# Hybrid encoder layer on one core: two units between the seven-product pairs, and four pieces of VectorE and ScalarE work that move to later steps

## The chip, the cores and the metric

The kernel runs on one core of one Trainium2 chip. The metric is the device time of one execution, in microseconds (us), as the median of several runs. The engines have short names in the profile: PE is TensorE (the matmuls), PEld its weight loads, DVE is VectorE, ACT is ScalarE, POOL is GpSimd and SP is the sync engine, which here issues nearly all loads.

## The reference

One layer of a streaming encoder on a sequence of 256 tokens, in float32. A token-mixing sub-layer (a gated recurrence, chunked attention and a state-space branch) comes first and is not touched by the change. After it comes the part that matters here:

```python
x = x + merged @ w_out[l]                       # 2048 x 2048
h = rmsnorm(x, norm_ffn_g[l])                   # the second norm
x = x + (jax.nn.silu(h @ w_ffn_gate[l]) * (h @ w_ffn_up[l])) @ w_ffn_down[l]
return rmsnorm(x, norm_final_g)                 # the last norm
# rmsnorm(x, g): x * rsqrt(mean(x*x) + 1e-6) * g
```

x has 256 rows (two halves of 128) and 2048 columns, w_ffn_gate and w_ffn_up have 2048 x 5632 elements, and w_ffn_down 5632 x 2048.

## The kernel before

**Units and steps.** Every large matmul is cut into units. A unit is two chunks of 128 rows of a weight matrix by 512 columns (512 KB). The main loop at the end of `trunk` takes one unit per step. Because float32 accuracy is wanted from a faster matmul type, each weight w is split into `hi` (a rounded copy, made by ACT) and `lo = w - hi` (made by DVE), and each product is three matmuls: x_hi by hi, x_lo by hi, x_hi by lo. A plain ("classic") unit is four products (two chunks, two halves of tokens), so 12 matmuls of 512 columns.

**The order inside a step.** At step d the loop issues the load of unit d+5, the `hi` part of unit d+2 on ACT, then the functions put off to this step with `later(n, fn)`, then the body of unit d (the matmuls on PE), then the functions of `later_pe(n, fn)`, and last the `lo` part of unit d+2 on DVE. This program order is the order of every engine's queue: nothing is rescheduled. So an ACT or DVE instruction that has to wait holds up all that was issued behind it. `hi` and `lo` have three buffers each (`PARTB`), raw weights four (`RAWB`).

**Seven-product pairs.** In the feed-forward part (`seven_block`) some units come in pairs p0, p1, p2 that use a seven-product scheme (as Strassen's) in place of eight products: the first unit of a pair has 9 matmuls and the second 12. A pair needs more DVE work than two classic units: `Pair.mix` and `Pair.low` form differences of raw weights (tiles `praw` to `mix`), and their hi and lo (`pmix`, one buffer) as well as those of the weights used as they are. `Pair.mix` of a pair is issued three steps ahead, `Pair.high` and `Pair.low` two steps ahead. In the listings below, one pair on DVE reads: `mix<-praw`, `mix<-praw,mix` x2, `pmix<-mix,pmix`, `lo<-praw,hi` (128x512), `pmix<-mix,pmix`, `lo<-praw,hi` (128x1024).

**A feed-forward block** computes 512 hidden columns for all tokens in 16 steps. The string `FFN_ORDER` (or `FIRST_ORDER` for block 0) gives the order of its units: p for a pair's two units, g for a gate unit, u for an up unit. There are 11 blocks: 0 to 5 form part 0 and 6 to 10 part 1; after each part `down_block` multiplies the part's hidden values by w_ffn_down, with its own orders. Around the units, a block has this work, by the step in which it is issued:

- `sum1`, `sum2`, `sum3`, in the three steps after the last pair: they combine the pairs' products (tile `sg` from PSUM on ACT, adds on DVE). `after` in the code is the step after the last pair.
- `silu` at step 13: two DVE adds (`sg<-sg,mm`), each with a Silu on ACT.
- `product` at step 16, which is step 0 of the next block: two DVE adds (`acc<-acc,mm`) and then two multiplications by the norm's root and the Silu (`sg<-acc,rstd,sg`), the gating.
- `turn`: the gated values are transposed on PE (`at_ps`, four transposes of 128 x 128 at a time), in the next block at steps `after`+2 and `after`+3, and one step after each the split into `at` follows: a copy on ACT (`at<-at_ps`), and then the difference on DVE (`at<-at_ps,at`).

For the last block of a part, the transposes come at once in the `down_block`, since that uses them.

**Norms.** `square` takes the sums of squares for the second norm during the w_out product; `norm` and `rstd_of` form the root: a sum and a scale on DVE, a Sqrt on ACT, and five small DVE instructions that refine it (tiles `ss`, `scr`, `rstd`). `silu` and `product` need the result. For the last norm, `square_down` squares x by columns of 512 on ACT and then multiplies x by the gain on DVE (`x<-x,gf`). The last 10 units (`last_body`) run the first token half alone, 6 matmuls a step, and then the whole second half at once.

Of the kernel before, what the change touches and what calls it, by code (L numbers as in the profile page):

```python
# [33 lines left out]
NORM_STEP = 14  # L34
LOAD_XA = 7
NQ = 3
FFN_ORDER = 'p0 p0 g p1 p1 u p2 p2 u g g g g u u u'
FIRST_ORDER = 'g g g u u u p0 p0 g p1 p1 g g u u u'
DOWN_ORDER = ('g g g g u u u u p0 p0 g p1 p1 u p2 p2 g g g g u u u u',
              'g g g g u u u p0 p0 g p1 p1 u g g g u u u u')  # L40
# [85 lines left out]
def trunk(  # L126
# [57 lines left out]
            act.activation(dst_hi, src, AF.Identity, scale=scale)  # L184
            vec.scalar_tensor_tensor(dst_lo, src, scale, dst_hi.bitcast(F32), ALU.mult, ALU.subtract)

    def rstd_of(dst, ss, scr):

        v, t = scr[:, 0:2], scr[:, 2:4]
        vec.tensor_scalar(v, ss, 1.0 / D, EPS, ALU.mult, ALU.add)  # L190
        act.activation(t, v, AF.Sqrt)
        vec.reciprocal(dst, t)
        vec.tensor_mul(t, dst, dst)
        vec.tensor_mul(t, t, v)
        vec.tensor_scalar(t, t, -0.5, 1.5, ALU.mult, ALU.add)
        vec.tensor_mul(dst, dst, t)

    def expacc(dst, src, tmp):

# [757 lines left out]
    fx = {}  # L957
# [41 lines left out]
    for n in range(4):  # L999
        cs = slice(n * 512, (n + 1) * 512)  # L1000

        def evac_out(acc, n=n, cs=cs):
            def add():
                x2 = fx["x2"]
                for h in range(2):
                    vec.scalar_tensor_tensor(x2[:, h, cs], acc[h], 0.5, x2[:, h, cs], ALU.mult, ALU.add)
                later(1, square)
                later_pe(1, turn)

            def square():  # L1010
                sq = tp.tile([P, 2, 512], F32, tag="t", name="sq")
                for h in range(2):
                    act.activation(sq[:, h, :], fx["x2"][:, h, cs], AF.Square, accum_out=ss4[:, h, n:n + 1])
                if n == 3:
                    def norm():
                        vec.tensor_reduce(ss, ss4, AX.X, ALU.add)
                        rstd_of(rstd2, ss, scr)
                    later(1, norm)

            def turn():  # L1020
                for k0 in (4 * n, 4 * n + 2):
                    t = transpose_tokens(lambda h, k: fx["x2"][:, h, k * P:(k + 1) * P], k0, "h2_ps")

                    def parts(k0=k0, t=t):
                        h2h, h2l = fx["h2"]
                        if k0 < 2 * NQ:
                            left_sums(k0, t)
                            return
                        for i in range(2):
                            split(h2h[:, k0 + i, :], h2l[:, k0 + i, :], t[:, i * S:(i + 1) * S],  # L1030
                                  prm[:, R_G2 + k0 + i:R_G2 + k0 + i + 1])
                    later(1, parts)
            later(1, add)
        add_job(w_out, KT, n * 512, as_body(lambda: mt[0], evac_out), after_mix if n == 0 else None)
# [166 lines left out]
    def ffn_block(part, n, n0, n1):  # L1201
        def silu(b):
            t = b["sg"]
            for h in range(2):
                vec.tensor_add(t[:, h, :], t[:, h, :], b["d"][2 * h])
                act.activation(t[:, h, :], t[:, h, :], AF.Silu, scale=rstd2[:, h:h + 1])

        def product(b):
            t, u = b["sg"], fx["acc"]
            for h in range(2):  # L1210
                vec.tensor_add(u[:, h, :], u[:, h, :], b["d"][2 * h + 1])
            for h in range(2):
                vec.scalar_tensor_tensor(t[:, h, :], u[:, h, :], rstd2[:, h:h + 1], t[:, h, :], ALU.mult, ALU.mult)
            fx["turn"] = lambda k0s=(0, 2): turn(b, k0s)
            if n == n1 - 1:
                later_pe(1, fx.pop("turn"))

        def turn(b, k0s):
            kb = 4 * (n - n0)
            if part not in at:  # L1220
                at[part] = tuple(fx["fp"].tile([P, 24, S], F32R, tag=f"at{i}", name=f"at{i}") for i in range(2))
            for k0 in k0s:
                tt = transpose_tokens(lambda h, k: b["sg"][:, h, k * P:(k + 1) * P], k0, "at_ps")
                v = tt.rearrange("p (k s) -> p k s", k=2)
                ks = slice(kb + k0, kb + k0 + 2)
                later(1, lambda ks=ks, v=v: split(at[part][0][:, ks, :], at[part][1][:, ks, :], v))

        def pre(b):
            def turns():
                t = fx.pop("turn", None)  # L1230
                if t is not None:
                    t((0,))
                    later_pe(1, lambda: t((2,)))
            later_pe(b["after"] + 2, turns)

        seven_block(FIRST_ORDER if n == 0 else FFN_ORDER, KT, [(w_gate, n * 512), (w_up, n * 512)],
                    lambda: fx["h2"], lambda p: fx["sum"][:, p], (sum1, sum2, sum3), (silu, product), pre)

    def down_block(part, c, n0, n1):

        src = w_down[n0 * 512:n1 * 512]
        order = DOWN_ORDER[part]
        n_pairs = len({o for o in order.split() if o[0] == "p"})
        cg, cu = (slice((c + i) * 512, (c + i + 1) * 512) for i in range(2))

        def sum_a(b):
            x2, u = fx["x2"], fx["acc"]
            act.copy(u[:, 0], b["p1"])
            vec.tensor_add(x2[:, 0, cg], x2[:, 0, cg], u[:, 0])
            vec.tensor_add(u[:, 0], u[:, 0], b["p67"][:, 0])  # L1250

        def sum_b(b):
            x2, u = fx["x2"], fx["acc"]
            vec.tensor_add(u[:, 1], u[:, 0], b["p67"][:, 1])
            vec.tensor_add(x2[:, 1, cg], x2[:, 1, cg], u[:, 1])

        def sum_c(b):
            u = fx["acc"]
            for h in range(2):
                vec.tensor_add(u[:, h], u[:, h], b["p5"])  # L1260

        def sum_d(b):
            vec.tensor_add(fx["x2"][:, :, cu], fx["x2"][:, :, cu], fx["acc"])

        def done(col):
            def fn(b):
                x2 = fx["x2"]
                cs = (cg, cu)[col]
                for h in range(2):
                    vec.tensor_add(x2[:, h, cs], x2[:, h, cs], b["d"][2 * h + col])  # L1270
                if part == 1:
                    later(1, lambda: square_down(c + col))
            return fn

        def left(p):

            ah, al = at[part]
            w = tp.tile([P, 2, 512], F32, tag="t", name="lw")
            a = w[:, 0, :].rearrange("p (k s) -> p k s", k=2)
            sf = w[:, 1, :].rearrange("p (i s) -> p i s", i=4)  # L1280
            ks = slice(2 * p, 2 * p + 2)
            vec.tensor_add(a, ah[:, ks, :].bitcast(F32), al[:, ks, :].bitcast(F32))
            a11, a21, a12, a22 = a[:, 0, :P], a[:, 0, P:], a[:, 1, :P], a[:, 1, P:]
            vec.tensor_add(sf[:, 0], a21, a22)
            vec.tensor_sub(sf[:, 1], sf[:, 0], a11)
            vec.tensor_sub(sf[:, 2], a11, a21)
            vec.tensor_sub(sf[:, 3], a12, sf[:, 1])

            def low():
                if p < 2:  # L1290
                    t = fx["fp"].tile([P, 2, 4, P], F32R, tag="sg", name="dsum", bufs=2)
                else:
                    t = fx["sum"][:, NQ]
                dsum[part, p] = t
                act.copy(t[:, 0], sf)
                vec.tensor_sub(t[:, 1], sf, t[:, 0].bitcast(F32))
            later(1, low)

        def pre(b):
            if c == 0:  # L1300
                for p in range(n_pairs):
                    later(1 + p, lambda p=p: left(p))
                if part == 1:
                    later_pe(2, load_gain)

        seven_block(order, 4 * (n1 - n0), [(src, c * 512), (src, (c + 1) * 512)], lambda: at[part],
                    lambda p: dsum[part, p], (sum_a, sum_b, sum_c, sum_d), (done(0), done(1)), pre)
# [3 lines left out]
    def square_down(c):  # L1311
# [1 line left out]
        cs = slice(c * 512, (c + 1) * 512)  # L1313
        sq = tp.tile([P, 2, 512], F32, tag="t", name="sq")
        for h in range(2):
            act.activation(sq[:, h, :], x2[:, h, cs], AF.Square, accum_out=sq3[:, h, c:c + 1])

        def scale():
            for h in range(2):
                vec.tensor_mul(x2[:, h, cs], x2[:, h, cs], fx["gf"][:, 0, cs])  # L1320
                if c == 2:
                    vec.tensor_reduce(sq3[:, h, 3:4], sq3[:, h, 0:3], AX.X, ALU.add)
                    vec.tensor_scalar(sq3[:, h, 3:4], sq3[:, h, 3:4], 1.0 / D, EPS, ALU.mult, ALU.add)
        later(1, scale)

    for part, (n0, n1) in enumerate(parts):
        for n in range(n0, n1):
# [5 lines left out]
        else:  # L1333
            def evac_down(acc):
                def add():
                    x2 = fx["x2"]
                    for h in range(2):
                        vec.tensor_add(x2[:, h, 1024:1536], x2[:, h, 1024:1536], acc[h])
                    later(1, lambda: square_down(2))
                later(1, add)  # L1340
            add_job(src, kt, 1024, as_body(lambda: at[1], evac_down))

# [173 lines left out]
```

## Time and profile before

| what | value |
|---|---|
| median of 3 runs | 1570.06 us (1570.06 to 1571.58) |
| the profiled execution's own time | 1568.95 us |
| its span, first to last instruction | 1567.1 us |
| granted TensorE clock | 0.998 |
| PE busy | 1552.4 us, 7073 matmuls |
| DVE busy | 1265.2 us |
| ACT busy | 889.8 us |

In the profiled execution the w_out product ends at about 848 us; blocks 0 to 5 run to 1105.6, the first down part to 1231.9, blocks 6 to 10 to 1447.4, and the last 10 units begin at 1528.0.

A matmul's end in the profile is modelled, and matmuls overlap: one of 512 columns is shown as 0.39 us long but the next can start 0.23 us after it. PE's busy share therefore hides waits shorter than the difference; they are found from the starts of one matmul and the next. On DVE and ACT, back-to-back instructions also overlap by about 0.1 us, so the cost of one is the distance from its start to the next start.

### The profile page before, as it was taken

To read this page: it belongs to the slowest core of one execution; us is meant where nothing else is said; L and a number is where in the kernel's file an instruction comes from. 1 tells how busy PE (TensorE), PEld (TensorE's weight loads), DVE (VectorE), ACT (ScalarE), POOL (GpSimd) and SP (SyncE) were. 2 spreads that over 40 slices of the span, in tenths; PEclk is the share of its full clock that TensorE was granted. 3 is DMA by queue.
4 is the path that set the end of the run, shared out by engine and by line. 5 is a ranking of instruction groups with operands and counts; after the bars stand their busy time and mean duration, and the time that the engine had idled before them with its cause. 6 is when DMAs were issued, how large, how long until landed. Compare 5 with 4: busy or idle time off the path is not lost.

```text
span 1567.1 us, 19709 instructions
## 1 busy us (share of the span) xinstructions
PE 1552.4 (99%) x7073; PEld 1272.9 (81%) x7073; DVE 1265.2 (81%) x1534; ACT 889.8 (57%) x1162; POOL 39.9 (3%) x88
## 2 busy tenths in 40 slices
PE   9999999999999999999999999999999999999997
PEld 7888888888888888888888788888888888888885
DVE  5876789988799999556666988888977988888964
ACT  6678575557677654544455555555545554545543
POOL 0011000000000000000000000000000000000000
PEclk9999999999999999999999999999999999999999
DMA  9678757787587766665656565564656666655663
GB/s 343 226 231 228 248 176 220 196 210 193 160 224 190 202 210 192 195 189 184 243 185 224 179 201 187 189 214 156 222 171 203 196 208 208 208 192 167 216 198 128
DMA packets 169842, 317.77 MB, mean 203 GB/s; under 512 B 11904, under 2 KB 24720, under 8 KB 168848
## 3 DMA queue, kind: packets, MB, share of 16 engines
q1 hardware_dynamic: 154624, 295.52, 59.0%
q0 software_dynamic: 11264, 10.49, 4.0%
q10 hardware_dynamic: 3856, 10.51, 1.8%
q8 instruction: 55, 0.90, 0.2%
q14 instruction: 43, 0.35, 0.1%
HBM read 310.17 MB, written 6.30 MB: 202 GB/s over the span
## 4 chain that ended last, share of the span: by engine, by line
PE 87%; DVE 9%; issue 2%; DMA 1%; ACT 1%; ACTq 0%; DVEq 0%; POOL 0%; SPq 0%; POOLq 0%
PE mm L82 77%; PE p L82 5%; DVE lo L82 3%; DVE mix L82 2%; DVE pmix L82 2%; DVE sg L82 1%; DVE acc L82 1%; DMA praw<-in_w_ffn_gate 1%; PE fm_ps L82 1%; PE y_ps L82 1%; PE bu L82 0%; PE lru_ps L82 0%; PE at_ps L82 0%; ACT hi L82 0%; PE o_ps L82 0%
## 5 line engine op out<-in xcount | busy, mean ns | idle before, releaser
L82 ACT CAST hi<-raw 128x1024 fp32r<-128x1024 f32 (+1 forms) x466 | 487.0, 1048 | 516.7 <-PE mm L82 451.8
L82 DVE TENSOR_TENSOR lo<-raw,hi 128x1024 fp32r<-128x1024 f32 (+1 forms) x466 | 563.0, 1214 | 146.7 <-ACT hi L82 145.0
L82 PE MATMUL mm<-hi,xth 128*128 128x512 f32 x768 | 303.7, 396 | 0.0
L82 PE MATMUL mm<-lo,xth 128*128 128x512 f32 x768 | 299.9, 391 | 0.0
L82 PE MATMUL mm<-hi,xtl 128*128 128x512 f32 x768 | 299.4, 390 | 0.0
L82 PE MATMUL mm<-hi,h2h 128*128 128x512 f32 x480 | 188.5, 393 | 0.0
L82 PE MATMUL mm<-lo,h2h 128*128 128x512 f32 x480 | 187.3, 390 | 0.7 <-DVE lo L82 0.6
L82 PE MATMUL mm<-hi,h2l 128*128 128x512 f32 x480 | 186.9, 389 | 0.0
L82 PEld LDWEIGHTS mm<-hi,xth 128*128 128x128 f32 x768 | 144.4, 188 | 32.4 <-ACT hi L82 2.6
L82 PEld LDWEIGHTS mm<-lo,xth 128*128 128x128 f32 x768 | 144.3, 188 | 31.9 <-DVE lo L82 1.5
L82 PEld LDWEIGHTS mm<-hi,xtl 128*128 128x128 f32 x768 | 144.6, 188 | 28.8
L82 PE MATMUL mm<-hi,at 128*128 128x512 f32 x528 | 162.9, 390 | 0.3 <-ACT hi L82 0.3
L82 ACT CAST pmix<-mix 128x1024 fp32r<-128x1024 f32 x80 | 84.1, 1051 | 120.8 <-DVE mix L82 113.3
L82 PEld LDWEIGHTS mm<-hi,at 128*128 128x128 f32 x528 | 98.9, 188 | 21.1 <-ACT hi L82 0.7
L82 PEld LDWEIGHTS mm<-lo,h2h 128*128 128x128 f32 x480 | 90.1, 188 | 20.4 <-DVE lo L82 1.5
L82 PEld LDWEIGHTS mm<-hi,h2l 128*128 128x128 f32 x480 | 90.1, 188 | 18.2
L82 PEld LDWEIGHTS mm<-hi,h2h 128*128 128x128 f32 x480 | 90.2, 188 | 18.1
L82 PE MATMUL mm<-lo,at 128*128 128x512 f32 x264 | 102.9, 390 | 0.5 <-DVE lo L82 0.5
L82 DVE TENSOR_TENSOR pmix<-mix,pmix 128x1024 fp32r<-128x1024 f32 x80 | 97.4, 1217 | 0.0
L82 PE MATMUL p<-pmix,lsum 128*128 128x512 f32 x306 | 85.2, 397 | 2.6 <-DVE pmix L82 2.6
L82 PE MATMUL mm<-hi,yc 128*128 128x512 f32 x256 | 79.0, 390 | 0.0
L82 DVE TENSOR_TENSOR lo<-praw,hi 128x512 fp32r<-128x512 f32 x80 | 76.0, 950 | 0.0
(232 smaller groups left out, 2051.4 us busy)
## 6 DMA issues: line engine op xcount, KB each, us to landing
raw<-in_w_in SPq DMA_DIRECT2D x190, 512.0 KB, 4.2
raw<-in_w_ffn_down SPq DMA_DIRECT2D x72, 512.0 KB, 4.8
raw<-in_w_ffn_gate SPq DMA_DIRECT2D x56, 512.0 KB, 5.9
raw<-in_w_ffn_up SPq DMA_DIRECT2D x56, 512.0 KB, 5.1
raw<-in_w_branch SPq DMA_DIRECT2D x48, 512.0 KB, 4.7
raw<-in_w_out SPq DMA_DIRECT2D x32, 512.0 KB, 4.7
praw<-in_w_ffn_gate SPq DMA_DIRECT2D x64, 256.0 KB, 5.7
praw<-in_w_ffn_up SPq DMA_DIRECT2D x64, 256.0 KB, 5.6
```

The lines of the kernel that those rows point to most:

```text
L82: return fn(*args, **kw)
```

## The change

Four edits. `FFN_ORDER` gets two classic units between p0 and p1 and between p1 and p2, where there was one. With that the last pair ends two steps later, so `after` is 10 where it was 8, and `sum1` to `sum3`, the transposes of `turn` and the splits behind them are issued two steps later. The gating in `product` is issued three steps later (one step later in the last block of a part). The second norm is issued two steps later, and its refinement three steps behind its Sqrt. In `square_down` the two squares are issued two steps apart, and the two multiplications come one per step, three or four steps later than before. No instruction is added or removed.

```diff
-FFN_ORDER = 'p0 p0 g p1 p1 u p2 p2 u g g g g u u u'
+FFN_ORDER = 'p0 p0 g g p1 p1 g u p2 p2 u g g u u u'
...
-    def rstd_of(dst, ss, scr):
+    def rstd_of(dst, ss, scr, wait=0):
 
         v, t = scr[:, 0:2], scr[:, 2:4]
         vec.tensor_scalar(v, ss, 1.0 / D, EPS, ALU.mult, ALU.add)
         act.activation(t, v, AF.Sqrt)
-        vec.reciprocal(dst, t)
-        vec.tensor_mul(t, dst, dst)
-        vec.tensor_mul(t, t, v)
-        vec.tensor_scalar(t, t, -0.5, 1.5, ALU.mult, ALU.add)
-        vec.tensor_mul(dst, dst, t)
+
+        def refine():
+            vec.reciprocal(dst, t)
+            vec.tensor_mul(t, dst, dst)
+            vec.tensor_mul(t, t, v)
+            vec.tensor_scalar(t, t, -0.5, 1.5, ALU.mult, ALU.add)
+            vec.tensor_mul(dst, dst, t)
+        if wait:
+            later(wait, refine)
+        else:
+            refine()
...
                 if n == 3:
                     def norm():
                         vec.tensor_reduce(ss, ss4, AX.X, ALU.add)
-                        rstd_of(rstd2, ss, scr)
-                    later(1, norm)
+                        rstd_of(rstd2, ss, scr, 3)
+                    later(3, norm)
...
             for h in range(2):
                 vec.tensor_add(u[:, h, :], u[:, h, :], b["d"][2 * h + 1])
-            for h in range(2):
-                vec.scalar_tensor_tensor(t[:, h, :], u[:, h, :], rstd2[:, h:h + 1], t[:, h, :], ALU.mult, ALU.mult)
-            fx["turn"] = lambda k0s=(0, 2): turn(b, k0s)
-            if n == n1 - 1:
-                later_pe(1, fx.pop("turn"))
+
+            def gate():
+                for h in range(2):
+                    vec.scalar_tensor_tensor(t[:, h, :], u[:, h, :], rstd2[:, h:h + 1], t[:, h, :], ALU.mult, ALU.mult)
+                fx["turn"] = lambda k0s=(0, 2): turn(b, k0s)
+                if n == n1 - 1:
+                    later_pe(1, fx.pop("turn"))
+            later(1 if n == n1 - 1 else 3, gate)
...
                 if part == 1:
-                    later(1, lambda: square_down(c + col))
+                    later_pe(0, lambda: square_down(c + col))
...
         for h in range(2):
-            act.activation(sq[:, h, :], x2[:, h, cs], AF.Square, accum_out=sq3[:, h, c:c + 1])
-
-        def scale():
-            for h in range(2):
+            later(1 + 2 * h, lambda h=h: act.activation(sq[:, h, :], x2[:, h, cs], AF.Square, accum_out=sq3[:, h, c:c + 1]))
+
+        def scale(h):
+            if True:
                 vec.tensor_mul(x2[:, h, cs], x2[:, h, cs], fx["gf"][:, 0, cs])
...
-        later(1, scale)
+        for h in range(2):
+            later(5 + h, lambda h=h: scale(h))
...
-                    later(1, lambda: square_down(2))
+                    later_pe(0, lambda: square_down(2))
```

How the order of instructions changes at three places follows. In the listings a row is one instruction, or several alike in a row (x2); `at_7640` and `at_7641` (`at_7674` and `at_7675` in the changed kernel) are the hi and lo tiles that hold the transposed hidden values.

DVE, from a block's third sum (step 10 before) to the next block's first classic unit. Before:

```order
L82 TENSOR_TENSOR acc<-sg,p_7769 128x512
L82 TENSOR_TENSOR lo<-raw,hi 128x1024
L82 TENSOR_TENSOR at_7641<-at_ps,at_7640 128x512
L82 TENSOR_TENSOR lo<-raw,hi 128x1024
L82 TENSOR_TENSOR at_7641<-at_ps,at_7640 128x512
L82 TENSOR_TENSOR lo<-raw,hi 128x1024
L82 TENSOR_TENSOR sg<-sg,mm 128x512 x2
L82 TENSOR_TENSOR lo<-raw,hi 128x1024
L82 TENSOR_TENSOR mix<-praw 128x1024
L82 TENSOR_TENSOR mix<-praw,mix 128x512 x2
L82 TENSOR_TENSOR pmix<-mix,pmix 128x1024
L82 TENSOR_TENSOR lo<-praw,hi 128x512
```

And in the changed kernel, from the third sum (step 12 now):

```order
L82 TENSOR_TENSOR acc<-sg,p_7765 128x512
L82 TENSOR_TENSOR lo<-raw,hi 128x1024
L82 TENSOR_TENSOR sg<-sg,mm 128x512 x2
L82 TENSOR_TENSOR at_7675<-at_ps,at_7674 128x512
L82 TENSOR_TENSOR lo<-raw,hi 128x1024
L82 TENSOR_TENSOR mix<-praw 128x1024
L82 TENSOR_TENSOR at_7675<-at_ps,at_7674 128x512
L82 TENSOR_TENSOR mix<-praw,mix 128x512 x2
L82 TENSOR_TENSOR pmix<-mix,pmix 128x1024
L82 TENSOR_TENSOR lo<-praw,hi 128x512
```

The two `at` differences stood at steps 11 and 12, ahead of the Silu's adds; they now stand at steps 13 and 14, the second of them inside the first pair of the next block, between `mix<-praw` and what follows from it.

ACT, from the copy of the first sum (`sg<-p`, step 8 before, 10 now) to the next block's first pair. Before:

```order
L82 COPY sg<-p_7770 128x512
L82 CAST hi<-raw 128x1024 x3
L82 CAST at_7640<-at_ps 128x512
L82 CAST hi<-raw 128x1024
L82 CAST at_7640<-at_ps 128x512
L82 CAST hi<-raw 128x1024
L82 ACTIVATE sg<-sg,rstd_108 128x512 x2
```

And in the changed kernel:

```order
L82 COPY sg<-p_7766 128x512
L82 CAST hi<-raw 128x1024 x3
L82 ACTIVATE sg<-sg,rstd_108 128x512 x2
L82 CAST at_7674<-at_ps 128x512
L82 CAST pmix<-mix 128x1024
L82 CAST hi<-praw 128x512
L82 CAST at_7674<-at_ps 128x512
L82 CAST pmix<-mix 128x1024
L82 CAST hi<-praw 128x1024
```

The copies into `at` moved with the transposes: the first stands behind the two Silu, the second behind the two casts of the next block's first pair, of which the first (`pmix<-mix`) reads what DVE's `mix<-praw` writes.

DVE, in the last 10 units (`res` is the kept hi and lo of units 30 to 37, `x` the residual, `gf` the gain of the last norm). Before:

```order
L82 TENSOR_TENSOR res<-raw,res 128x1024 x2
L82 TENSOR_TENSOR x_6433<-x_6433,gf 128x512
L82 TENSOR_REDUCE sq_109<-sq_109 128x1
L82 TENSOR_SCALAR sq_109<-sq_109 128x1
L82 TENSOR_TENSOR x_6433<-x_6433,gf 128x512
L82 TENSOR_REDUCE sq_109<-sq_109 128x1
L82 TENSOR_SCALAR sq_109<-sq_109 128x1
L82 TENSOR_TENSOR res<-raw,res 128x1024 x4
L82 TENSOR_TENSOR lo<-raw,hi 128x1024 x2
```

And in the changed kernel:

```order
L82 TENSOR_TENSOR res<-raw,res 128x1024 x5
L82 TENSOR_TENSOR x_6433<-x_6433,gf 128x512
L82 TENSOR_REDUCE sq_109<-sq_109 128x1
L82 TENSOR_SCALAR sq_109<-sq_109 128x1
L82 TENSOR_TENSOR res<-raw,res 128x1024
L82 TENSOR_TENSOR x_6433<-x_6433,gf 128x512
L82 TENSOR_REDUCE sq_109<-sq_109 128x1
L82 TENSOR_SCALAR sq_109<-sq_109 128x1
L82 TENSOR_TENSOR lo<-raw,hi 128x1024 x2
```

The two multiplications moved behind three more `lo` parts, and one `lo` part stands between them.

## The prediction

> **What bounds the kernel now.** The page comes first: busy time, granted clock, and the chain that ended last.
>
> ```profile
> PE 1552.4 (99%) x7073; PEld 1272.9 (81%) x7073; DVE 1265.2 (81%) x1534; ACT 889.8 (57%) x1162; POOL 39.9 (3%) x88
> PEclk9999999999999999999999999999999999999999
> PE 87%; DVE 9%; issue 2%; DMA 1%; ACT 1%; ACTq 0%; DVEq 0%; POOL 0%; SPq 0%; POOLq 0%
> ```
>
> PE sets the time, at full clock. The 9% of DVE in the chain is where the change works: places in which PE's next operand is DVE's last product. The chain in order of time (start, length) gives the rhythm of a block:
>
> ```profile
> 984.15 2.56 PE p L82 x10
> 994.46 10.20 PE mm L82 x45
> 1027.41 2.56 PE p L82 x10
> ```
>
> 45 matmuls take 10.20 us, 0.227 each, so a classic step takes 2.72 us and a pair 2.04 + 2.72. A block takes 1027.41 - 984.15 = 43.26 us. The timeline of PE shows what else is in it:
>
> ```profile
> 961.24 0.60 PE L82 MATMUL at_ps<-cst,sg 128*128 128x128 f32 x4
> ...
> 961.91 0.39 PE L82 MATMUL mm<-hi,h2l 128*128 128x512 f32 x1
> ...
> 983.26 0.61 PE L82 MATMUL p<-pmix,lsum 128*128 128x512 f32 x2
> 984.15 0.96 PE L82 MATMUL p<-pmix,lsum 128*128 128x512 f32 x3 [0.27 <-DVE pmix L82]
> ...
> 991.31 1.77 PE L82 MATMUL p<-pmix,lsum 128*128 128x512 f32 x6
> ```
>
> Four transposes and one matmul take 0.67 (961.24 to 961.91), so a group of transposes adds 0.45. A block's 183 matmuls and two groups are 41.5 + 0.9 = 42.4; 0.8 is waiting. It lies at p1, where the third matmul, the first that needs the low part of `pmix`, starts 0.89 after 983.26 in place of 0.45, with a second gap of 0.12 behind it (0.96 for three, 0.84 without), and at p2 (1.77 for six, 1.53 without): 0.44 + 0.12 + 0.24 = 0.8. So a wait costs its length and about 0.11 more.
>
> Why DVE is late there, in its own timeline:
>
> ```profile
> 962.82 0.69 DVE L82 TENSOR_TENSOR at<-at_ps,at 128x512 fp32r<-128x512 f32 x1 [2.02 <-ACT at L82]
> 963.43 1.22 DVE L82 TENSOR_TENSOR lo<-raw,hi 128x1024 fp32r<-128x1024 f32 x1
> ...
> 967.71 1.28 DVE L82 TENSOR_TENSOR sg<-sg,mm 128x512 f32<-128x512 f32 x2
> 968.90 1.22 DVE L82 TENSOR_TENSOR lo<-raw,hi 128x1024 fp32r<-128x1024 f32 x1
> 970.04 1.22 DVE L82 TENSOR_TENSOR mix<-praw 128x1024 f32<-128x1024 f32 x1
> 971.29 1.42 DVE L82 TENSOR_TENSOR mix<-praw,mix 128x512 f32<-128x512 f32 x2
> 972.62 1.22 DVE L82 TENSOR_TENSOR pmix<-mix,pmix 128x1024 fp32r<-128x1024 f32 x1
> 973.76 0.68 DVE L82 TENSOR_TENSOR lo<-praw,hi 128x512 fp32r<-128x512 f32 x1
> 974.36 1.22 DVE L82 TENSOR_TENSOR pmix<-mix,pmix 128x1024 fp32r<-128x1024 f32 x1
> ...
> 976.63 1.27 DVE L82 TENSOR_TENSOR acc<-acc,mm 128x512 f32<-128x512 f32 x2
> 977.83 1.41 DVE L82 SCALAR_TENSOR_TENSOR sg<-acc,rstd,sg 128x512 f32<-128x512 f32 x2
> 979.15 1.22 DVE L82 TENSOR_TENSOR lo<-raw,hi 128x1024 fp32r<-128x1024 f32 x1
> ```
>
> From 967.71 on no row has idle time. By starts, a pair costs DVE 1.25 + 1.33 + 1.14 + 0.60 + 2 x 1.14 = 6.6 us against 4.76 on PE; a classic unit 1.14 against 2.72; product adds 1.20, gating 1.32 and an `at` 0.61. With one classic unit between pairs and gating in the way, DVE falls behind at p1. What it waits for (2.02 for an `at`) does no harm at steps 11 and 12, where only classic units follow.
>
> **The change part by part.** *Spacing and gating* free that stretch: two classic units give DVE 5.4 - 2.3 = 3.2 us of slack against a pair's deficit of 1.8. In blocks whose predecessor made no transposes (1 and 7), I let DVE run without waits: the Silu's adds end 1.1 after E (below), the first pair's two units are ready by E+8.8, the product's adds done by E+10.0, p1's first low part by E+16.1; PE needs that at E+18.8. No wait is left. What goes away there, and at the second norm, from PE's rows and one of DVE:
>
> ```profile
> 852.50 0.17 DVE L82 RECIPROCAL rstd<-scr 128x2 f32<-128x2 f32 x1 [2.67 <-ACT scr L82]
> ...
> 856.46 0.39 PE L82 MATMUL mm<-hi,h2l 128*128 128x512 f32 x1
> 857.48 0.50 PE L82 MATMUL mm<-lo,h2h 128*128 128x512 f32 x1 [0.63 <-DVE lo L82]
> ...
> 893.45 0.39 PE L82 MATMUL mm<-hi,h2l 128*128 128x512 f32 x1
> 893.91 0.50 PE L82 MATMUL mm<-lo,h2h 128*128 128x512 f32 x1
> ...
> 896.33 0.63 PE L82 MATMUL p<-pmix,lsum 128*128 128x512 f32 x2
> 897.63 1.20 PE L82 MATMUL p<-pmix,lsum 128*128 128x512 f32 x4 [0.67 <-DVE pmix L82]
> ...
> 1281.94 1.63 PE L82 MATMUL p<-pmix,lsum 128*128 128x512 f32 x5
> ...
> 1289.79 1.51 PE L82 MATMUL p<-pmix,lsum 128*128 128x512 f32 x5
> ```
>
> Each is the distance over its norm, plus 0.11. Block 1: 893.45 to 893.91 gives 0.23 + 0.11, 896.33 to 897.63 (0.45 without a wait) 0.85 + 0.11, its p2 as elsewhere 0.24: 1.5 us. Block 7: five matmuls take 1.30 without a wait, so 0.33 + 0.21 = 0.5.
>
> *Second norm.* DVE sat 2.67 us behind the Sqrt and its table load, and the `lo` behind it made PE wait 1.02 - 0.23 + 0.11 = 0.9. Two steps later, its reduction is followed by pair work that doesn't need the Sqrt, and the refinement comes when that is done: 0.9 saved. The Sqrt and table load now hold ACT ahead of p0's second cast, and the refinement DVE ahead of p1, both for less than that 2.67; p1's low part lands within 0.1 of when it is needed, and I allow 0.2 for it.
>
> *Transposes and splits two steps later.* This is the edit that I expect to cost most. Let E be the end of step 12's products on PE (967.6 in the block shown, where the Silu's adds stand at the same step). ACT's rows:
>
> ```profile
> 962.20 0.58 ACT L82 CAST at<-at_ps 128x512 fp32r<-128x512 f32 x1
> ...
> 967.59 1.06 ACT L82 CAST hi<-raw 128x1024 fp32r<-128x1024 f32 x1 [1.66 <-PE mm L82]
> 968.56 1.33 ACT L82 ACTIVATE sg<-sg,rstd 128x512 f32<-128x512 f32 x2
> 971.29 1.05 ACT L82 CAST pmix<-mix 128x1024 fp32r<-128x1024 f32 x1 [1.40 <-DVE mix L82]
> 972.24 0.62 ACT L82 CAST hi<-praw 128x512 fp32r<-128x512 f32 x1
> ```
>
> In the new order ACT runs hi (0.97 to the next start), two Silu (1.24), then the first `at` copy, done at E+2.8 (0.97 + 1.24 + 0.58). DVE, idle since its adds, does the first `at` difference (0.61), `lo` (1.14) and `mix` (1.25), done at E+5.8. Only now can ACT cast `pmix` (0.95) and `hi` (0.53), and only behind them copy the second `at` (0.58): E+7.9. DVE waits 2.1 us with all of p0 behind it, then does `at` (0.61), two differences (1.33) and the low part (1.22): E+11.05. PE reaches p0 at E + 3 x 2.72 + 2 x 0.45 = E+9.06 and needs the low part with its third matmul at E+9.5. It waits 1.55 + 0.11 = 1.7.
>
> DVE then runs without a break, and PE meets it twice more. It ends p0's second unit, the adds and step 2's `lo` at E+16.3; PE, 1.7 late, needs it at E+15.95: 0.35 + 0.11. `lo`, `mix`, p1's first unit (end of its low part E+21.1, needed E+21.9) and the gating follow, and the low part of p1's second unit at E+24.2; needed at E+23.9: 0.3 + 0.1. Sum: 1.7 + 0.5 + 0.4 = 2.6 us, once in each block whose predecessor issued transposes: 2 to 5 and 8 to 10, seven blocks. The 0.8 of before goes in each. In blocks 5 and 10 classic units of the down part follow, which have the time (as at 963.43).
>
> *One step more in the last block of a part.* In the down part the gating and the two `at` each move one step later past one `lo`; what stands ahead of a given `lo` two steps on is the same. I take 0.
>
> *Last norm.* DVE's and PE's rows from the last ten units:
>
> ```profile
> 1531.50 0.69 DVE L82 TENSOR_TENSOR x<-x,gf 128x512 f32<-128x512 f32 x1
> ...
> 1533.21 2.36 DVE L82 TENSOR_TENSOR res<-raw,res 128x1024 fp32r<-128x1024 f32 x2
> ...
> 1541.74 0.50 PE L82 MATMUL mm<-lo,at 128*128 128x512 f32 x1 [0.52 <-DVE lo L82]
> ```
>
> The products and small sums took DVE 1.71 us ahead of two `lo` parts, whose ends free raw buffers for the last two loads. Later they let these loads start up to 1.7 earlier, and stand as 0.85 each ahead of the last `lo` parts, when a step lasts 1.36. Bounds -1.7 and +1.7; the same work stands ahead of the last `lo`, so I take +0.2. The squares (ACT, 57% busy) cost nothing.
>
> Sum: gone are 1.5 + 0.5 + 0.9 + 7 x 0.8 = 8.5; new are 7 x 2.6 + 0.2 + 0.2 = 18.6. Net +10.1. The profiled execution took 1568.95 us (span 1567.1): 1579.0. It lies 1.1 below the median shown; as a median, 1580.
>
> **The rivals.** *Only the new wait costs (slower by less).* The second and third waits have margins of 0.3 us, behind eleven DVE instructions; were each 0.03 shorter, both would vanish: 7 x 1.7 + 0.4 - 8.5 = +3.8, 1574.
>
> *The splits stay hidden (faster).* If the second `at` reached DVE by E+6.3 in place of E+7.9, as it would if ACT could copy it ahead of the pair's casts, PE would find p0 ready: -8.5 + 0.4, 1562. For it: 3.3 us of such waits cost nothing before. Against: they now stand behind `mix`, and ACT takes its queue in order in every row above.
>
> *Gain and loss cancel (no change).* At 1.2 us a block in place of 2.6, 7 x 1.2 equals the 8.5: 1570. That needs the first wait cut to 1.1 and the others hidden.
>
> *The lag spreads to p2.* Its low part has 1.2 us of margin by the same sums; with 1 us more per block, 1587.
>
> *The clock.* The granted clock stays at 9 tenths or more over waits of up to 0.85; waits of 1.7 are not in the trace, and if with them seven blocks of 45 us ran at 0.9, the least that a 9 in that row stands for, it would cost 7 x 5 = 35 us: 1614. The Trainium skill warns of this: its page "TensorE: Matmul & The Clock Gate", section "HAM oscillation — how this bites in real kernels", has PE fall to half its clock after idle gaps beyond about 3.4 us, and the section after it has frequent short idles do the same. By that limit of length the clock stays, and the trace agrees for waits up to 0.85.
>
> **How the numbers follow.** Chances: forecast 0.74, only the new wait 0.11, hidden 0.06, cancelled 0.04, spread 0.04, clock 0.01. The forecast's own range is 1577 to 1584 (0.15 on each of some twenty waits, and the last norm's bounds). For 8 in 10 it reaches 1573, which takes in most of the first rival, and 1586. A measurement here tells 0.2% (3.1 us) from no change. Faster has 0.06; same 0.06 (cancelled, and 0.02 of the first rival); slower 0.88.
>
> **What would show it.** After: DVE's `mix` followed by an idle of about 2.1 us before the second `at`, released by ACT; PE waiting for `pmix` at p0, not p1 or p2, with blocks 45.1 us long where they were 43.26; blocks 1, 6 and 7 without a wait, at 42 us; no DVE wait behind the Sqrt. I am wrong if blocks 2 to 5 keep 43.3 us or less, or if the wait at p0 is under 1 us.

## The result and the profile after

The changed kernel takes 1578.92 us (median of four, 1578.57 to 1580.4) against 1570.32 us for the kernel before (median of four): a ratio of 1.0061, with a 95% interval of 1.0049 to 1.0073. It is slower by 0.6%, about three times what can be told from no change. Its profiled execution took 1579.03 us, with a span of 1577.2; before, the span was 1567.1. The spans differ by 10.1 us.

The page of the changed kernel, the three lines that were shown of before:

```profile
PE 1552.6 (98%) x7073; PEld 1272.5 (81%) x7073; DVE 1266.0 (80%) x1534; ACT 891.1 (56%) x1162; POOL 39.8 (3%) x88
PEclk9999999999999999999999999999999999999999
PE 88%; DVE 5%; issue 2%; DMA 2%; ACT 2%; SPq 0%; ACTq 0%; POOL 0%; DVEq 0%
```

The work is the same and PE is as busy as before (1552.6 and 1552.4 us); the span grew by idle time alone. The granted clock is 0.998 in both. DVE's share of the chain fell from 9% to 5% although the waits grew, and ACT's rose from 1% to 2%. So the shares of the chain don't tell whether a change has helped. The chain in order of time does:

```profile
998.36 2.72 PE p L82 x12
...
1043.33 2.72 PE p L82 x12
```

The same place in two blocks one after the other: 1043.33 - 998.36 = 44.97 us a block, where it was 43.26. What PE waits for in such a block, from its timeline:

```profile
975.25 0.61 PE L82 MATMUL p<-pmix,lsum 128*128 128x512 f32 x2
977.24 1.20 PE L82 MATMUL p<-pmix,lsum 128*128 128x512 f32 x4 [1.37 <-DVE pmix L82]
...
981.91 0.39 PE L82 MATMUL mm<-hi,h2l 128*128 128x512 f32 x1
982.44 0.50 PE L82 MATMUL mm<-lo,h2h 128*128 128x512 f32 x1
...
989.61 1.25 PE L82 MATMUL p<-pmix,lsum 128*128 128x512 f32 x3
```

There are three waits. At p0 the third matmul starts 1.99 us after the pair in place of 0.45: 1.53 of wait (by exact starts), and 0.11 for the gap one matmul later. At the `lo` of step 2: 0.53 in place of 0.23, 0.30 and 0.11. At p1's second unit: 1.25 for three matmuls in place of 0.84, 0.41 in all. Together 2.46 us. The view of PE's waits, summed over the run, has the first of them seven times:

```profile
PE p L82 <- DVE pmix L82: 9.6, 7, 1.4
```

Why PE waits, in DVE's timeline of the same block. E, the end of step 12's products, is 966.16, when the `hi` cast that waits for them starts on ACT:

```profile
965.67 1.37 DVE L82 TENSOR_TENSOR sg<-sg,mm 128x512 f32<-128x512 f32 x2
968.95 0.69 DVE L82 TENSOR_TENSOR at<-at_ps,at 128x512 fp32r<-128x512 f32 x1 [1.92 <-ACT at L82]
969.56 1.22 DVE L82 TENSOR_TENSOR lo<-raw,hi 128x1024 fp32r<-128x1024 f32 x1
970.69 1.22 DVE L82 TENSOR_TENSOR mix<-praw 128x1024 f32<-128x1024 f32 x1
974.03 0.69 DVE L82 TENSOR_TENSOR at<-at_ps,at 128x512 fp32r<-128x512 f32 x1 [2.12 <-ACT at L82]
974.64 1.41 DVE L82 TENSOR_TENSOR mix<-praw,mix 128x512 f32<-128x512 f32 x2
975.96 1.22 DVE L82 TENSOR_TENSOR pmix<-mix,pmix 128x1024 fp32r<-128x1024 f32 x1
...
981.17 2.35 DVE L82 TENSOR_TENSOR lo<-raw,hi 128x1024 fp32r<-128x1024 f32 x2
...
989.09 1.22 DVE L82 TENSOR_TENSOR pmix<-mix,pmix 128x1024 fp32r<-128x1024 f32 x1
```

And in ACT's:

```profile
966.16 1.05 ACT L82 CAST hi<-raw 128x1024 fp32r<-128x1024 f32 x1 [1.71 <-PE mm L82]
967.12 1.33 ACT L82 ACTIVATE sg<-sg,rstd 128x512 f32<-128x512 f32 x2
968.36 0.57 ACT L82 CAST at<-at_ps 128x512 fp32r<-128x512 f32 x1
971.95 1.05 ACT L82 CAST pmix<-mix 128x1024 fp32r<-128x1024 f32 x1 [3.02 <-DVE mix L82]
972.90 0.62 ACT L82 CAST hi<-praw 128x512 fp32r<-128x512 f32 x1
973.42 0.58 ACT L82 CAST at<-at_ps 128x512 fp32r<-128x512 f32 x1
```

Read the two together. ACT stands idle for 3.02 us, because the next instruction in its queue, the cast of `pmix`, needs DVE's `mix`. The copy into `at` behind that cast could have run in that time: its transposes end on PE at 969.94, 2 us before that cast begins. DVE then stands idle for 2.12 us, because its next instruction needs that copy. Each engine waits once for the other, and the pair that PE needs next stands behind both.

The root of the second norm holds DVE up no more. The refinement follows without idle time:

```profile
865.20 1.22 DVE L82 TENSOR_TENSOR mix<-praw 128x1024 f32<-128x1024 f32 x1
866.33 0.16 DVE L82 RECIPROCAL rstd<-scr 128x2 f32<-128x2 f32 x1
...
867.20 1.41 DVE L82 TENSOR_TENSOR mix<-praw,mix 128x512 f32<-128x512 f32 x2
```

### The profile page after: what moved, and what is told of

Read it like the earlier page. It is cut to its first block, busy times and chain, and to the rows that moved or that the text cites. A ratio compares the mean times of both kernels' runs of the same rounds, so it can differ in the third digit from the quotient of the medians.

```text
span 1577.2 us, 19643 instructions
## 1 busy us (share of the span) xinstructions
PE 1552.6 (98%) x7073; PEld 1272.5 (81%) x7073; DVE 1266.0 (80%) x1534; ACT 891.1 (56%) x1162; POOL 39.8 (3%) x88
## 4 chain that ended last, share of the span: by engine, by line
PE 88%; DVE 5%; issue 2%; DMA 2%; ACT 2%; SPq 0%; ACTq 0%; POOL 0%; DVEq 0%
PE mm L82 80%; PE p L82 5%; DVE lo L82 1%; DVE pmix L82 1%; DVE mix L82 1%; DMA praw<-in_w_ffn_up 1%; ACT hi L82 1%; PE fm_ps L82 1%; DVE sg L82 1%; PE y_ps L82 1%; PE bu L82 0%; PE lru_ps L82 0%; DMA raw<-in_w_ffn_down 0%; DVE acc L82 0%; PE o_ps L82 0%
## 5 line engine op out<-in xcount | busy, mean ns | idle before, releaser
L82 PEld LDWEIGHTS p<-pmix,lsum 128*128 128x128 f32 x306 | 56.8, 188 | 28.0 <-DVE pmix L82 16.9
```

Of the source, the lines that this page charges most:

```text
L82: return fn(*args, **kw)
```

## The experiments

The theory: the whole loss comes from the second copy into `at`, which ACT reaches only behind the pair's casts. Without it the change would be a gain. The rivals: DVE simply has too much work there, wherever the copy stands; or another of the edits is at fault. The suspected cause was therefore taken away alone (e1). The gating and each norm were undone (e3, e5, e6), and the late transposes and the late gating were also done alone (e4, e7). The two units between the pairs were neither undone nor done alone; what they are worth is read from a difference (under e4).

Totals of two executions differ by up to 2.8 us at the start, and by about 1 us at the end, for reasons that no edit touches: the first matmul on `hi` of the feed-forward part began at 843.8 to 846.6 us in the ten traces, though the code up to there is the same. For an edit inside the feed-forward part the sharper measure is one stretch of the trace, from that matmul to the first one that uses `res`. These two rows, of the changed kernel, give its two ends; they come from the view of PE by tiles, with three durations in ns (least, median, most) of each group, and then the starts of its first and last matmul:

```profile
L82 PE MATMUL mm<-hi,h2h x480: 387/389/481, 844.4 to 1455.7; 128*128 128x512 f32 x160
L82 PE MATMUL mm<-res,at x96: 389/389/499, 1537.6 to 1564.7; 128*128 128x512 f32 x96
```

The stretch is 1537.6 - 844.4 = 693.2 us. For all kernels:

| kernel | stretch, us | median, us | ratio to before (95%) |
|---|---|---|---|
| before | 684.0 | 1570.32 | |
| after | 693.2 | 1578.92 | 1.0061 (1.0049 to 1.0073) |
| e1, second copy first | 677.7 | 1563.03 | 0.9962 (0.9948 to 0.9977) |
| e2, e1 and gating two steps later | 675.3 | 1560.39 | 0.9946 (0.9930 to 0.9963) |
| e3, after with the gating back | 699.7 | 1585.19, one run | |
| e4, before with late transposes alone | 710.6 | 1596.14, one run | |
| e5, after with the second norm back | 693.8 | 1579.03, one run | |
| e6, after with the last norm back | 693.1 | 1580.91, one run | |
| e7, before with late gating alone | 683.9 | 1568.22, one run | |
| e8, e2 and both norms later still | 674.9 | 1559.84 | 0.9944 (0.9931 to 0.9958) |

Stretches are differences of rows that are rounded to 0.1 us. The ratios of e1, e2 and e8 are to runs of the kernel before that go with them (medians of 1569.06 us for e1 to e4 and 1569.24 us for e5 to e8), that of the changed kernel to the 1570.32 us. The experiments with one run have a trace and no interval; they are read by their stretch and their waits.

### e1: the second copy ahead of the pair's casts

ACT's copy of the second `at` is issued at the head of the same step, ahead of the casts (a list `early`, run before that step's high parts). DVE's difference stays where it was. No other instruction moves.

```diff
-    late, late_pe = {}, {}
+    late, late_pe, early = {}, {}, {}
...
+    def sooner(n, fn):
+
+        early.setdefault(state["done"] + n, []).append(fn)
...
-                later(1, lambda ks=ks, v=v: split(at[part][0][:, ks, :], at[part][1][:, ks, :], v))
+                if k0s == (2,):
+                    sooner(1, lambda ks=ks, v=v: act.copy(at[part][0][:, ks, :], v))
+                    later(1, lambda ks=ks, v=v: vec.tensor_sub(at[part][1][:, ks, :], v, at[part][0][:, ks, :].bitcast(F32)))
+                else:
+                    later(1, lambda ks=ks, v=v: split(at[part][0][:, ks, :], at[part][1][:, ks, :], v))
...
+        for fn in early.pop(d, ()):
+            fn()
```

> The changed kernel, with one ACT instruction moved: the second `at` copy is issued ahead of the casts of the next block's first pair, in the same step, and not behind them. Theory A (the copy's place behind the casts, which read DVE's `mix`, makes DVE wait 2.1 us with all of p0 behind it): the wait of DVE before the second `at` goes, PE's waits at p0 (1.64 us) and at step 2 (0.42) go, and of the third at p1 some 0.3 to 0.5 stays, since the gating still stands ahead of p1's second unit. Seven blocks gain about 2 us each: 1564 to 1566 us, faster than the kernel before. Rival B (the two units between the pairs, or the later gating, make PE wait, and the copy's place only shows it): PE still waits over 1 us at p0, 1575 us or more.

Measured: 1563.03 us, 0.9962 of before: the change of place of one ACT instruction per block turns a loss of 0.6% into a gain of 0.4%. ACT's timeline, and then DVE's, at the place of the listings above:

```profile
966.57 0.57 ACT L82 CAST at<-at_ps 128x512 fp32r<-128x512 f32 x1
968.19 0.59 ACT L82 CAST at<-at_ps 128x512 fp32r<-128x512 f32 x1 [1.06 <-PE at_ps L82]
970.16 1.05 ACT L82 CAST pmix<-mix 128x1024 fp32r<-128x1024 f32 x1 [1.38 <-DVE mix L82]
```

```profile
968.91 1.22 DVE L82 TENSOR_TENSOR mix<-praw 128x1024 f32<-128x1024 f32 x1
970.04 0.68 DVE L82 TENSOR_TENSOR at<-at_ps,at 128x512 fp32r<-128x512 f32 x1
970.64 1.41 DVE L82 TENSOR_TENSOR mix<-praw,mix 128x512 f32<-128x512 f32 x2
```

ACT now waits 1.06 us for the transposes, copies, and only then waits 1.38 us for `mix`. The copy ends at 968.78, well ahead of the difference that needs it at 970.04; DVE's 2.12 us are gone. With them went the waits at p0 and at step 2, of which only the first is directly behind the copy. What is left is 0.21 + 0.11 at p1's second unit, and the block takes 42.76 us in the chain:

```profile
986.37 0.50 PE p L82
...
1029.13 0.50 PE p L82
```

The theory holds, and the rival that DVE has too much work there is left with 0.32 us a block. The total came 1 us below the expected range, which was reckoned from the changed kernel's 1579 us; the kernel before took 1569.06 us beside these runs, in place of 1570.32.

### e2: the gating two steps later still

```diff
-            later(1 if n == n1 - 1 else 3, gate)
+            later(1 if n == n1 - 1 else 5, gate)
```

This is on top of e1.

> As the run with the copy moved, and the gating two steps later still (five steps after the product and not three), behind all of p1's low parts. Theory A: no wait of PE over 0.15 us is left in any feed-forward block but block 0, blocks take 42.4 us, and seven blocks gain all 2.46 us: 1579 - 17.2 = 1562 us. Rival B: the gating's place is without effect or makes it worse, 1565 us or more.

Measured: 1560.39 us, and a stretch 2.4 us shorter than e1's. Of this 7 x 0.33 = 2.3 is the blocks, 42.43 us against 42.76. The wait at p1 is gone, and all rows of the chain from one p1 to the next are PE's own:

```profile
983.34 2.72 PE p L82 x12
986.06 7.48 PE mm L82 x33
...
1025.77 2.72 PE p L82 x12
```

1025.77 - 983.34 = 42.43 us, the 42.4 that the matmuls and transposes alone take. No `PE p` row is left among PE's waits in this kernel; by the starts of the matmuls, block 0 keeps 0.19 + 0.11 us at its p1, as expected.

### e3: the gating back

```diff
-            later(1 if n == n1 - 1 else 3, gate)
+            gate()
```

> The changed kernel with the gating back in the product's step. Theory A, by starts on DVE: the wait at p0 stays 1.64 us, the `lo` of step 2 comes 1.32 us later, so the wait there grows from 0.42 to about 1.7, and the wait at p1's second unit goes: 3.4 us per block in place of 2.46, 1579 + 7 x 0.95 = 1585 to 1586 us; blocks 1 and 7 stay without a wait. Rival B (the later gating is what costs): faster than the changed kernel.

Measured: 1585.19 us, a stretch 6.5 us longer than after's. PE's waits:

```profile
PE mm L82 <- DVE lo L82: 10.6, 8, 1.5
PE p L82 <- DVE pmix L82: 9.5, 7, 1.4
```

The wait at p0 is as it was. The one at step 2 grew from 0.30 to 1.64 a block, and the one at p1 is gone. That is 1.64 + 1.75 = 3.39 a block, 0.93 more, and 7 x 0.93 = 6.5. One thing was not expected: block 1, which was to stay without a wait, has 0.24 + 0.11 us at the `lo` of its step 2, which the gating of block 0 now stands ahead of. So the late gating was worth 0.9 us a block in the changed kernel: it moved 1.32 us of DVE work from a place ahead of the step-2 `lo`, at which all of it was paid, to one ahead of p1's second unit, at which 0.4 of it was.

### e4: only the transposes and splits later

The kernel before, its order and gating as they were, with `turn` at `after` + 4 in place of + 2.

```diff
-            later_pe(b["after"] + 2, turns)
+            later_pe(b["after"] + 4, turns)
```

> The kernel before with one edit: the transposes and the splits behind them two steps later, as the change has them, all else as before. Theory A: the two `at` stand at steps 13 and 14, DVE waits 2.1 us for the second, and with the old spacing and gating PE waits at p0, at the unit after it and at p1, about 4.7 us per block in seven blocks in place of 0.8: 1570 + 27 = 1590 to 1600 us. Rival B (it costs only together with the new order): 1568 to 1573 us.

Measured: 1596.14 us, a stretch 26.6 us longer than before's. DVE's timeline has the same idle time as in the changed kernel, behind the same `mix`:

```profile
975.04 1.22 DVE L82 TENSOR_TENSOR mix<-praw 128x1024 f32<-128x1024 f32 x1
978.38 0.69 DVE L82 TENSOR_TENSOR at<-at_ps,at 128x512 fp32r<-128x512 f32 x1 [2.12 <-ACT at L82]
```

With one unit between pairs DVE never recovers, and PE waits at p0 (1.48), step 2 (1.64), p1 (0.82) and p2 (0.12), each with its 0.11 or so:

```profile
PE p L82 <- DVE pmix L82: 14.5, 15, 1.3
PE mm L82 <- DVE lo L82: 11.7, 10, 1.5
```

Per block this is 3.8 us more than before (47.06 against 43.26 from the chain), in seven blocks 26.6. The edit that the prediction called the costliest is so on its own too, and the other edits, the two units and the late gating above all, took back 710.6 - 693.2 = 17.4 us of it. How that splits follows from e3, which differs from this kernel by the two units and the norms: 710.6 - 699.7 = 10.9 us, of which the second norm is 0.6 (e5). That leaves some 10 us for the two units, and 6.5 for the gating.

### e5: the second norm back

```diff
-                        rstd_of(rstd2, ss, scr, 3)
-                    later(3, norm)
+                        rstd_of(rstd2, ss, scr)
+                    later(1, norm)
```

> The changed kernel with the second norm as before: issued two steps earlier, its refinement right behind the Sqrt. Theory A: DVE waits some 2.7 us for the Sqrt again and PE 0.8 + 0.1 us for the `lo` behind it (at about 857 us); PE's 0.3 us at p1 of block 0 (at about 869 us) goes. Net 0.6 us slower than the changed kernel, 1579.5 us. Rival B (the norm's wait was hidden by what DVE had ready): no wait there, no difference.

Measured: a stretch of 693.8 us, 0.6 longer than after's. The wait of 0.80 + 0.11 us at the first `lo` of block 0 is back, and the 0.19 + 0.11 at block 0's p1 is gone: 0.9 - 0.3 = 0.6. Its total, 1579.03 us, equals the changed kernel's profiled one; 0.6 us can't be seen there.

### e6: the last norm back

The squares and multiplications of `square_down` and the places from which it is called are as before.

```diff
-            later(1 + 2 * h, lambda h=h: act.activation(sq[:, h, :], x2[:, h, cs], AF.Square, accum_out=sq3[:, h, c:c + 1]))
+            act.activation(sq[:, h, :], x2[:, h, cs], AF.Square, accum_out=sq3[:, h, c:c + 1])
...
-        for h in range(2):
-            later(5 + h, lambda h=h: scale(h))
+        later(1, scale)
```

> The changed kernel with the last norm as before: both squares in one step, both multiplications in the next. PE's waits in the last ten units were 2.0 us before and 2.8 in the changed kernel, 1.9 to 2.4 in other runs with the new last norm. Theory A (the last norm's edit starts loads earlier, but they land no earlier, and its multiplications delay the last `lo`): 1.8 to 2.1 us of waits, up to 0.8 us faster. Rival B (the difference is from run to run): 1.8 to 2.8 us, no pattern.

Measured: 1580.91 us. Of the two us above the changed kernel, all lie ahead of the stretch: its first matmul on `hi` came at 846.6 in place of 844.4. The stretch is the same (693.1 and 693.2). In the last units PE waited 2.73 us in all, against 2.80 in the changed kernel and 1.98 in the kernel before, so putting the old order back did not bring the 1.98 back. By the starts of the matmuls, the four traces with the old order have 1.8 to 2.7 us of waits there and the five with the new one 2.0 to 3.0; the 1.9 to 2.4 of the expectation was too narrow. From the first matmul on `res` to the last matmul, the four traces with the old order took 28.95 to 29.81 us (mean 29.4) and the five with the new one 29.09 to 30.05 (mean 29.6). A difference of 0.2 inside a spread of 1 can't be told from none. The edit did nothing to the time that these runs can show; what it did to the loads is told at the end.

### e7: only the gating later

The kernel before, with its gating three steps later (one in the last block of a part), as in the changed kernel.

> The kernel before with one edit: the gating three steps later, all else as before. Theory A (DVE is behind over the whole stretch from p0 to p2, and an instruction moved inside the stretch only moves the wait): PE's wait at p1 (0.55 us) goes, that at p2 grows from 0.23 to about 0.8, and the time stays within 1 us of the kernel before. Rival B (the gating ahead of p1 is itself the cause of the waits): both waits go or shrink, up to 0.8 us in each of eight blocks, 1563 to 1565 us.

Measured: a stretch of 683.9 against 684.0 us, and a block of 43.24 against 43.26:

```profile
991.41 2.56 PE p L82 x10
1034.65 2.57 PE p L82 x10
```

```profile
PE p L82 <- DVE pmix L82: 4.7, 9, 0.7
```

The wait at p1 (0.43 + 0.11 before) is gone, and the one at p2 grew to 0.68 + 0.11: the same 0.8 a block one pair later. With one unit between pairs, DVE is short of time in the whole stretch, and moving 1.32 us of work within it moves only the place of the wait.

### e8: e2 with both norms later still

The refinement of the second norm five steps behind its root in place of three, and the last block of multiplications of the last norm behind the last `lo` parts.

```diff
-                        rstd_of(rstd2, ss, scr, 3)
+                        rstd_of(rstd2, ss, scr, 5)
...
-            later(5 + h, lambda h=h: scale(h))
+            later((8 if c == 2 else 5) + h, lambda h=h: scale(h))
```

> As the run with the copy moved and the gating five steps later (1560.4 us), and two more: the second norm's refinement five steps behind its Sqrt in place of three, and the last norm's two multiplications of the third column group three steps later, behind the last `lo`. Theory A: PE's 0.3 us at p1 of block 0 goes, and of the waits in the last ten units some 0.6: 1559.5 us, which beats both kernels. Rival B (both are hidden or the waits move on): 1560.4 us.

Measured: 1559.84 us, 0.9944 of before. It is the fastest of these kernels and beats both; against e2 (0.9946) the total tells nothing, but the trace does. Block 0's wait of 0.19 + 0.11 us at p1 is gone, with a stretch 0.3 us shorter than e2's (by exact starts). The multiplications now stand behind the last `lo` parts: the second of these ends at 1532.89 on DVE, where the first multiplication starts at 1532.80. From the first matmul on `res` to the last matmul it took 27.97 us, below all nine others, with 0.70 + 0.11 + 0.11 us of waits. This is one trace, a microsecond below the lowest of nine that spread over 1.1. From the feed-forward part on, PE's view of waits has one row left, 0.5 us for a `res` part.

## Why the prediction was right

It was forecast slower, at 1580 us and +10.1 us of span; measured were 1578.92 us and +10.1. The agreement of the sum to the tenth is partly luck, as its terms show.

**The ledger of the late splits** holds step by step, read from the listings of DVE, ACT and PE above with E = 966.16:

| step | predicted | measured |
|---|---|---|
| first `at` copy done | E+2.8 | E+2.8 |
| `mix` done | E+5.8 | E+5.8 |
| second `at` copy done | E+7.9 | E+7.8 |
| DVE idle before the second `at` | 2.1 | 2.12 |
| p0's low part done | E+11.05 | E+11.0 |
| PE at p0 | E+9.06 | E+9.1 |
| step 2's `lo` done, needed | E+16.3, E+15.95 | E+16.2, E+16.0 |
| p1's last low part done | E+24.2 | E+24.15 |

It could be made from the kernel before because every duration in it stands in that trace, and only the order is new.

**The terms of the sum:**

| term | predicted, us | measured, us |
|---|---|---|
| p0, step 2, p1's second unit | 1.7, 0.5, 0.4 | 1.64, 0.41, 0.41 |
| in seven blocks | +18.2 | +17.2 |
| block 0's p1 behind the refinement | +0.2 | +0.3 |
| waits gone in blocks 1 to 5, 7 to 10 and at the second norm | -8.5 | -8.3 |
| sum inside the stretch | +9.9 | +9.2; the stretch grew by 9.2 |
| last norm, the end | +0.2 | +0.7 from the first matmul on `res` to the last |
| behind the last matmul | 0 | +0.2 |

Small misses cancel. The blocks' term was 0.14 a block too large, which is 1.0 us; the waits that go are 0.2 us less than forecast, and block 0's is 0.1 more. The end came out 0.5 longer, which lies inside the spread of that part in nine traces (e6). The last 0.2 us are the stores behind the last matmul: they were issued at the same distance from it and landed 8.1 in place of 7.9 us behind it. So the +0.2 for the last norm was neither confirmed nor refuted, and lay well inside its bounds.

**What goes away** was right. Blocks 1, 6 and 7 have no wait, and the 0.9 of the second norm is gone; e5 brought it back. The 0 taken for the last block of a part held too: PE has no wait in the down part behind either.

**The rivals.** "Only the new wait costs" needed the second and third waits, put at 0.35 and 0.3 us, to vanish: both came, each at 0.30 of wait and 0.11 of gap, so the case was as near as the prediction said. "The splits stay hidden" failed in the changed kernel, but its condition was the right one: e1 makes ACT copy ahead of the pair's casts, and it took 1563.03 us, where that rival's sum gave 1562. The sum lacked the 0.32 us a block that DVE's work still costs at p1. "Gain and loss cancel" needed the first wait to be 1.1 us and the others hidden, and they are 1.64, 0.41 and 0.41. "The lag spreads to p2" is excluded by PE's rows, which have no wait there. So is "the clock": the granted clock stayed at 0.998 with 21 waits of up to 1.5 us. By the limit of about 3.4 us that the Trainium skill gives (page "TensorE: Matmul & The Clock Gate", section "HAM oscillation — how this bites in real kernels") it was to stay, and the trace agrees for waits up to 1.64 us, the longest of e3 and e4, which also ran at 0.998. Three waits a block here, and four in e4, did not lower it either.

**What the prediction didn't weigh** is how far the parts depend on each other. It counted the two units and the late gating together as room for DVE; e7 shows the late gating worth nothing alone, and e3 shows it worth 0.9 us a block beside the late splits.

## What to carry to other kernels

An instruction moved across a step on two engines can meet a different neighbour on each of them: read both queues at the new place, and look for a pair in which A waits for B's product and B, behind that wait, has what A needs next. The remedy may be one instruction: here a copy went ahead of a cast whose input came 2 us later than its own, and a loss of 0.6% became a gain of 0.4%. On a saturated stretch a moved piece of work only moves the wait (e7); first make room, then move.

## What the runs showed that was not expected

**Loads issued earlier landed hardly earlier, and the one ahead of them landed later.** With the multiplications out of the way, the last two loads were issued 1.7 us sooner, as the prediction held possible for a gain of up to 1.7 us. The rows of SP's queue for the last four loads, of after and then of before:

```profile
1539.64 3.77 SPq L254 DMA_DIRECT2D raw<-in_w_ffn_down  x4
```

```profile
1530.47 5.50 SPq L248 DMA_DIRECT2D raw<-in_w_ffn_down  x4
```

They are issued within 3.77 in place of 5.50 us. In e6, with the old order back, it is 5.50 again. The last load landed 12.2 us after the first matmul on `res` in both kernels; over the traces it is 12.1 to 12.9 us in four with the old order (mean 12.4) and 11.6 to 12.5 in the five of the changed kernel, e1, e2, e3 and e5 (mean 12.1). So 1.7 us of earlier issue brought at most a few tenths.

The second of the four was issued at the same time in all ten, 3.19 us after that matmul. Its time from issue to landing, of after and then of before:

```profile
raw<-in_w_ffn_down SPq DMA_DIRECT2D x1, 512.0 KB, 6.5
```

```profile
raw<-in_w_ffn_down SPq DMA_DIRECT2D x1, 512.0 KB, 5.0
```

It landed at 7.4 to 8.2 us where the two loads behind it came at the old times, and at 8.3 to 9.9 in all six traces where they came sooner. PE's wait moved with it. The changed kernel waits for the `hi` part of this second load:

```profile
1548.37 0.73 PE L82 MATMUL mm<-res,at 128*128 128x512 f32 x2 [1.07 <-ACT res L82]
```

By starts that wait is 1.24 us. In the kernel before it came in time, and PE waits 0.47 us for the third load instead; e4 and e6, also with the old order, wait 1.13 and 1.52 us for the third. That loads in flight share what the path moves is inferred from these times; no run measured it apart.

**The start of the run moves by itself.** The first matmul on `hi` of the feed-forward part lay between 843.8 and 846.6 us in ten executions with the same code ahead of it. 2.8 us is 0.18% of the time, more than most of the edits here are worth; the stretch between two matmuls of the trace told kernels apart whose waits differ by 0.3 us (e2 and e8), where single totals could not.

**A wait of PE costs 0.11 us more than its length.** In all kernels a second gap of 0.107 to 0.115 us follows every wait of 0.18 to 1.64 us from the feed-forward part on, one matmul behind the first, however long the wait was. No run here shows what makes it.
